# Stores on another queue and a divided last product in an encoder step

## The chip, the cores and the metric

The kernel runs on one core of one Trainium2 chip. The metric is device time in microseconds of one execution; the profiled execution is a further one, whose records give the span and the rows that are quoted. Engines are named as in the profile: PE multiplies matrices, PEld loads its weights, DVE, ACT and POOL work elementwise, SP issues transfers. SP and POOL each have a program of their own: an instruction that waits holds up everything behind it on the same engine.

## The reference

One layer of a streaming encoder over 2048 prompt frames and 64 sample frames of width 1024: a gated linear recurrence and a windowed attention are merged, multiplied by an output projection and added to the input; then a convolutional feed-forward network with a down projection, and a final RMS norm. The parts around the change are:

```python
def rmsnorm(x, g):
    x32 = x.astype(jnp.float32)
    y = x32 * lax.rsqrt(jnp.mean(x32 * x32, axis=-1, keepdims=True) + RMS_EPS)
    return (y * g.astype(jnp.float32)).astype(x.dtype)
...
        mixed = jax.nn.sigmoid(g_rnn) * y_rnn + jax.nn.sigmoid(g_attn) * y_attn
        x = x + mixed @ w_out[l]
        xn2 = rmsnorm(x, norm_ffn[l])
        up = xn2 @ w_up[l]
        fbuf = jnp.zeros((b, FFN_CONV_W - 1, 2 * D_FF), x.dtype) if first else ffn_conv[l]
        up_c, fbuf_new = causal_dwconv(up, fbuf, ffn_conv_w[l], ffn_conv_b[l])
        gate, val = jnp.split(up_c, 2, axis=-1)
        x = x + (jax.nn.silu(gate) * val) @ w_down[l]
...
    y = rmsnorm(x, norm_final)
```

All is float32, with D_MODEL = 1024 and D_FF = 2816.

## The kernel before

Each float32 operand is split into a rounded part and a remainder (hi on ACT at L197, lo on DVE at L198), and each product is three matmuls: hi by hi, hi by lo, lo by hi. The 2112 frames are columns, cut into six blocks of 320, 320, 320, 320, 416 and 416; two of them are a pair, and PAIRS names the three pairs. SBUF is divided into regions (RA, RB, RC, RE, FW, FA, FB, FD and more), and the profile names tiles by their region: "RE<-woS" is a load of output-projection weights into RE.

The mixer (recurrence, attention) fills the first 1370 us. Three stages follow.

*Output projection, about 1373 to 1600.* Three phases, i = 0, 1, 2, one for each pair. In each, `wout(i, m)` makes eight row blocks m: it loads the residual of two tiles (L796, from xT), multiplies the mixed rows by the block's weights (`mm3`, L223 to L225: 48 matmuls), and `residual` adds (L811), squares (L815 or L818) and sums the squares (L819); the result goes to x1S in DRAM (L812). `wload(i, m)` gets the weights: in phase 0 from the input, split and stored to woS (L787); in phases 1 and 2 from woS (L780), 1 MB each into one of two buffers. `wload(i, m + 1)` stands after the matmuls in `wout`. Stores are put in a list, `stores`, and issued one `wout` later behind the next loads. `norms(i - 1)` makes the RMS factors of the pair before (L681 on PE, L682 on ACT, L683 on DVE) at m = 0. Beside all this a generator prepares the next pair's rows (`mixes`, loads at L772) and the feed-forward operands of a finished pair (`xprep`, loads of x1S at L733); `drive(beside, n)` lets it take n steps for each m.

*Up projection and convolution, about 1600 to 2555.* Products of a Strassen-like scheme, seven in place of eight, over 22 groups of rows and three pairs (a plan lists which lanes run together). Up weights are combined, split and stored for the next pass (wuS, L853) or loaded back; each lane's result goes through convolution and gate and is stored as operand of the down products (hS, L995).

*Down projection, about 2555 to 3022.* `seq` lists seven products by three pairs by 11 steps; each step loads one token tile of hS (`dtoken`, L1079), splits it, and does twelve matmuls (L1305 to L1307). The last product of the first pair, (6, 0), comes at the end and is done in two passes over its 11 steps, rows 0 and 1 and then rows 2 and 3; the second pass loads and splits the same 11 tiles again. Generators in `side`, driven one step after each product step, add the residual, square (L1276), sum (L1277), and write the outputs: `outputs` makes the RMS factor (L681 to L683), multiplies each of eight row blocks (L1286) and stores it (L1287).

No scheduler reorders this: the order on an engine is the order in which the Python code calls it, with the generators interleaved and a helper that delays some operations by a number of products (`later`). Every store and load of the whole kernel is issued by SP.

## Time and profile before

| | |
|---|---|
| median of 3 runs | 3022.07 us (3018.11 to 3022.51) |
| profiled execution | 3023.75 us, span 3022.0 us |
| PE busy | 2883.6 us, 95% |
| DVE, ACT, POOL busy | 2173.0, 1520.8, 146.2 us |
| granted TensorE clock | 0.98 |
| transfers | 581.14 MB, mean 192 GB/s |
| chain that ended last | PE 70%, DVE 11%, DMA 9%, ACT 3% |

The largest transfers that the change touches, from the page's list of issues (out <- in, issuing queue, count, KB each, median us from issue to landing):

```profile
hS<-FA SPq DMA_DIRECT2D x154, 160.0 KB, 3.1
hS<-FB SPq DMA_DIRECT2D x77, 208.0 KB, 4.2
woS<-RB SPq DMA_DIRECT2D x8, 1024.0 KB, 6.2
x1S<-FW SPq DMA_DIRECT2D x32, 160.0 KB, 5.5
out_yT_dram<-RR SPq DMA_DIRECT2D x32, 160.0 KB, 2.9
```

How to read rows: a group has line, engine, operation, tiles and count, then busy us and mean ns, then idle time ahead of it with what ended it. In waits the thing behind the arrow is what came last. "SPq" is time of SP's instruction stream, waits included, and a busy PE counts as busy at the slow clock too.

### The profile page before, as it was taken

The page shows a single profiled execution, that of the slowest core. Times are in us where ns is not written, and L with a number is a line of the kernel's source. Part 1 is how long each engine was busy: PE and PEld are TensorE (multiplying, and loading weights), DVE is VectorE, ACT ScalarE, POOL GpSimd, SP SyncE. Part 2 cuts the span into 40 slices and gives each one's busy share as a digit, 9 for nine tenths or more (in the row PEclk, how much of TensorE's full clock was granted, in tenths as well). Part 3 has the DMA queues.
Part 4 walks back from the last instruction along what each step waited for, and adds up shares of the span by engine and source line. Part 5 has one row for each costly group of instructions (what it writes and reads, how often), then busy time and mean ns, then how long its engine had stood idle before and what let it go on. Part 6 is the DMA issues. An engine that isn't in the chain of part 4 may idle for free.

```text
span 3022.0 us, 48591 instructions
## 1 busy us (share of the span) xinstructions
PE 2883.6 (95%) x17572; PEld 2797.1 (93%) x17572; DVE 2173.0 (72%) x4220; ACT 1520.8 (50%) x3427; POOL 146.2 (5%) x104
## 2 busy tenths in 40 slices
PE   8989999999999999999899999999699999999997
PEld 7989888999998999998799999999599999899997
DVE  5398884378786288886568888888866767566776
ACT  4466662366663366664325555555444545334442
POOL 3221112000000000000000000000000000000000
PEclk9999999999999999999899999999899999999998
DMA  7875537543335643338875555545767666976653
GB/s 240 279 233 179 188 134 232 193 134 125 124 122 167 201 138 129 125 106 279 274 245 204 183 176 179 177 166 189 252 213 240 225 229 217 269 215 203 210 171 125
DMA packets 340914, 581.14 MB, mean 192 GB/s; under 512 B 35169, under 2 KB 263841, under 8 KB 320705
## 3 DMA queue, kind: packets, MB, share of 16 engines
q1 hardware_dynamic: 340672, 578.04, 58.3%
q8 instruction: 138, 2.26, 0.3%
q14 instruction: 104, 0.84, 0.1%
HBM read 393.26 MB, written 185.18 MB: 191 GB/s over the span
## 4 chain that ended last, share of the span: by engine, by line
PE 70%; DVE 11%; DMA 9%; ACT 3%; issue 2%; SPq 1%; POOL 0%; DVEq 0%; ACTq 0%; POOLq 0%
PE mm L224 8%; PE mm L223 8%; PE mm L225 8%; PE mf L913 6%; PE mf L914 6%; PE mf L915 6%; PE mm L913 4%; PE mm L915 4%; PE mm L914 4%; PE mf L1306 2%; PE mf L1307 2%; PE mf L1305 2%; PE pt L467 1%; PE mm L1306 1%; PE mm L1307 1%
## 5 line engine op out<-in xcount | busy, mean ns | idle before, releaser
L223 PE MATMUL mm<-xh,whl 128*128 128x320 f32 (+2 forms) x2112 | 689.8, 327 | 8.7 <-ACT xh L197 5.6
L224 PE MATMUL mm<-xl,whl 128*128 128x320 f32 (+2 forms) x2112 | 688.3, 326 | 8.5 <-DVE xl L198 4.8
L225 PE MATMUL mm<-xh,whl 128*128 128x320 f32 (+2 forms) x2112 | 684.9, 324 | 0.8 <-POOL whl L198 0.8
L197 ACT ACTIVATE RE<-FW 128x512 fp32r<-128x512 f32 (+2 forms) x585 | 320.1, 562 | 446.9 <-DMA FW<-hS 68.7
L198 DVE TENSOR_TENSOR RE<-FW,RE 128x512 fp32r<-128x512 f32 (+2 forms) x585 | 344.4, 604 | 182.6 <-ACT RE L197 164.7
L224 PEld LDWEIGHTS mm<-xl,whl 128*128 128x128 f32 x2112 | 400.8, 190 | 17.8 <-DVE xl L198 8.2
L223 PEld LDWEIGHTS mm<-xh,whl 128*128 128x128 f32 x2112 | 401.1, 190 | 16.2 <-ACT xh L197 8.0
L225 PEld LDWEIGHTS mm<-xh,whl 128*128 128x128 f32 x2112 | 401.1, 190 | 1.8 <-POOL whl L198 1.1
L1306 PE MATMUL mf<-RE 128*128 128x320 f32 (+1 forms) x594 | 192.4, 324 | 1.9 <-DVE RE L198 1.8
L1305 PE MATMUL mf<-RE 128*128 128x320 f32 (+1 forms) x594 | 192.7, 325 | 0.0
L1307 PE MATMUL mf<-RE 128*128 128x320 f32 (+1 forms) x594 | 191.0, 322 | 0.0
L913 PE MATMUL mf<-RE 128*128 128x320 f32 (+1 forms) x472 | 155.0, 330 | 19.3 <-ACT RE L197 15.1
L949 DVE SCALAR_TENSOR_TENSOR FW<-FA,pkt,FW 128x640 f32<-128x640 f32 x176 | 154.4, 879 | 10.9 <-ACT FW L943 8.0
L915 PE MATMUL mf<-RE 128*128 128x320 f32 (+1 forms) x472 | 153.4, 326 | 2.1 <-DVE RE L198 2.1
L914 PE MATMUL mf<-RE 128*128 128x320 f32 (+1 forms) x472 | 154.1, 327 | 0.4 <-DVE RE L198 0.4
L913 PE MATMUL mm<-RE 128*128 128x320 f32 (+1 forms) x408 | 132.5, 325 | 5.6 <-DVE FA L966 2.8
L913 PE MATMUL mf<-RA,RE 128*128 128x320 f32 (+1 forms) x416 | 136.8, 329 | 0.0
L914 PE MATMUL mf<-RA,RE 128*128 128x320 f32 (+1 forms) x416 | 136.2, 327 | 0.0
L915 PE MATMUL mf<-RA,RE 128*128 128x320 f32 (+1 forms) x416 | 135.8, 326 | 0.0
L915 PE MATMUL mm<-RE 128*128 128x320 f32 (+1 forms) x408 | 131.5, 323 | 4.0 <-DVE RE L198 4.0
L914 PE MATMUL mm<-RE 128*128 128x320 f32 (+1 forms) x408 | 131.5, 322 | 0.0
L454 ACT ACTIVATE pr<-S,nm 128x256 f32<-128x256 f32 (+1 forms) x272 | 123.4, 472 | 7.5 <-DVE nm L450 6.0
(336 smaller groups left out, 7059.8 us busy)
## 6 DMA issues: line engine op xcount, KB each, us to landing
whl<-wiS SPq DMA_DIRECT2D x88, 1024.0 KB, 5.1
RE<-wuS SPq DMA_DIRECT2D x96, 512.0 KB, 4.3
wiS<-whl SPq DMA_DIRECT2D x44, 1024.0 KB, 4.8
wuS<-RE SPq DMA_DIRECT2D x88, 512.0 KB, 2.7
FW<-in_w_up_dram SPq DMA_DIRECT2D x160, 256.0 KB, 3.4
FW<-in_w_dn_dram SPq DMA_DIRECT2D x121, 256.0 KB, 4.1
FW<-hS SPq DMA_DIRECT2D x165, 160.0 KB, 3.3
hS<-FA SPq DMA_DIRECT2D x154, 160.0 KB, 3.1
```

Of the source, the lines that this page charges most:

```text
L197: nc.scalar.activation(hi, src, AF.Copy)
L198: (lo_eng or nc.vector).tensor_tensor(lo, src, hi.bitcast(F32), op=ALU.subtract)
L223: nc.tensor.matmul(ps[:, :n], wh[:, c], xh[:, k, :n], start=first, stop=False)
L224: nc.tensor.matmul(ps[:, :n], wh[:, c], xl[:, k, :n], start=False, stop=False)
L225: nc.tensor.matmul(ps[:, :n], wl[:, c], xh[:, k, :n], start=False, stop=last)
L913: nc.tensor.matmul(ps[:, :n], w[:, 0, c], x[:, k, 0], start=first, stop=False, **more)
L914: nc.tensor.matmul(ps[:, :n], w[:, 0, c], x[:, k, 1], start=False, stop=False, **more)
L915: nc.tensor.matmul(ps[:, :n], w[:, 1, c], x[:, k, 0], start=False, stop=last, **more)
L949: nc.vector.scalar_tensor_tensor(uc, G[:, j:j + self.cols], col("fw", 44 * j + m), uc, op0=ALU.mult, op1=ALU.add)
L1305: nc.tensor.matmul(ps[m][:, :n], w[:, 0, c], t[:, 0], start=k == 0, stop=False)
L1306: nc.tensor.matmul(ps[m][:, :n], w[:, 0, c], t[:, 1], start=False, stop=False)
L1307: nc.tensor.matmul(ps[m][:, :n], w[:, 1, c], t[:, 0], start=False, stop=k == 10)
```

## The change

Ten kinds of stores move from SP's queue to POOL's: the final states h, lc and fc, woS, x1S, wuS, hS, s2S, the sums rS, and the outputs yT. POOL has no other work after the mixer. The list of delayed stores disappears, so each store is issued where its result is made. `wload(i, m + 1)` moves to the start of `wout`, ahead of the residual's loads. `norms(i - 1)` moves to m = 1, and phase 2's generator takes no steps at m = 0 and 1 and three afterwards, in place of two each time.

The last product keeps its 11 token tiles after the first pass. Four of them are loaded and split early, at step (6, 1, 3), into buffers of up weights that are free by then (`wh`). Rows 2 and 3 are done in two column halves of 160 in place of one pass of 320; squares and outputs follow by column slice, and `outputs` yields three more times before its RMS factor.

```diff
-            stores.append(lambda: nc.sync.dma_start(woS[m], t.bitcast(F32)))
+            nc.gpsimd.dma_start(woS[m], t.bitcast(F32))
...
     def wout(i, m):
         w, work = weights.pop((i, m)), []
+        if m < 7:
+            wload(i, m + 1)
...
-        due = stores[:]
-        stores.clear()
-        if m < 7:
-            wload(i, m + 1)
-        for f in due:
-            f()
...
-            stores.append(lambda t0=t0, n=n, xr=xr: nc.sync.dma_start(x1S[m, :, t0:t0 + n], xr))
+            nc.gpsimd.dma_start(x1S[m, :, t0:t0 + n], xr)
...
-                nc.sync.dma_start(wuS[g, i], t.bitcast(F32))
+                nc.gpsimd.dma_start(wuS[g, i], t.bitcast(F32))
...
-                nc.sync.dma_start(hS[ORDER.index(o), g % 11, :, OFF[p]:OFF[p] + n], src)
+                nc.gpsimd.dma_start(hS[ORDER.index(o), g % 11, :, OFF[p]:OFF[p] + n], src)
...
-        t = dr.tile([P, 2, BM], F32R, name="hh")[:, :, :n]
+        t = (wh.tile([P, 2, 4 * P], F32R, name="wh") if spare else dr.tile([P, 2, BM], F32R, name="hh"))[:, :, :n]
...
-    seq += [(6, 0, k, r) for r in (range(2), range(2, 4)) for k in range(11)]
+    seq += [(6, 0, k, r, c) for r, c in ((range(2), slice(0, 320)), (range(2, 4), slice(0, 160)),
+                                         (range(2, 4), slice(160, 320))) for k in range(11)]
...
-            toks[j] = dtoken(prods[i][1], p, k)
+            if (i, p, k) not in toks:
+
+                toks[i, p, k] = dtoken(prods[i][1], p, k, (i, p) == (6, 0) and k < 4)
...
-            if i and m == 0:
+            if i and m == 1:
                 norms(i - 1)
...
-            drive(beside, (2, 4, 2)[i])
+            drive(beside, (2, 4, 3)[i] if i < 2 or m > 1 else 0)
...
-    def outputs(p, c):
+    def outputs(p, c, cs=None):
         b, n = PAIRS[p][c == "2"]
-        r = rms(ssum[b], n, ssum[b])
+        cs = cs or slice(0, n)
+        s = ssum[b][:, cs]
+        for _ in range(3):
+            yield
+        r = rms(s, cs.stop - cs.start, s)
...
-            nc.sync.dma_start(yT[m * P:(m + 1) * P, b:b + n], y)
+            nc.gpsimd.dma_start(yT[m * P:(m + 1) * P, b + cs.start:b + cs.stop], y)
...
+        if (i, p, k) == (6, 1, 3):
+            for jj in range(4):
+                fetch(len(seq) - 33 + jj)
```

SP at the end of phase 0, before (L772 mixed rows, L796 residual, L787 and L780 store and load of woS, L812 store of x1S):

```order
L772 DMA FW<-mixS 128x320 x2
L787 DMA woS<-RB 128x2048
L796 DMA FW<-in_xT_dram 128x320 x2
L812 DMA x1S<-FW 128x320 x2
L772 DMA FW<-mixS 128x320 x2
L780 DMA RE<-woS 128x2048
L812 DMA x1S<-FW 128x320 x2
L796 DMA FW<-in_xT_dram 128x320 x2
L780 DMA RE<-woS 128x2048
L772 DMA FW<-mixS 128x416 x2
```

And SP there in the changed kernel:

```order
L796 DMA FW<-in_xT_dram 128x320
L780 DMA RE<-woS 128x2048
L772 DMA FW<-mixS 128x320
L785 DMA FW<-in_w_out_dram 128x512
L796 DMA FW<-in_xT_dram 128x320
L772 DMA FW<-mixS 128x320
L785 DMA FW<-in_w_out_dram 128x512
L796 DMA FW<-in_xT_dram 128x320
L772 DMA FW<-mixS 128x320
L780 DMA RE<-woS 128x2048
L785 DMA FW<-in_w_out_dram 128x512
```

Both of phase 1's first loads of woS now stand among the loads of phase 0's own weights (L785), and no store stands in the queue.

DVE in the tail, before (L198 splits of token tiles, L1277 and L683 sums and RMS factor, L1333 sums of products, L1286 outputs):

```order
L683 RECIPROCAL FD<-FD 128x416
L1277 TENSOR_TENSOR FD<-FD 128x320
L1286 SCALAR_TENSOR_TENSOR RR<-RR,pkt,FD 128x416 x8
L683 RECIPROCAL FD<-FD 128x320
L198 TENSOR_TENSOR RE<-FW,RE 128x320
L1286 SCALAR_TENSOR_TENSOR RR<-RR,pkt,FD 128x320 x8
L198 TENSOR_TENSOR RE<-FW,RE 128x320 x5
L1333 TENSOR_TENSOR RR<-mm,RR 128x320 x2
```

And in the changed kernel, where the lines are L1272 for the sums, L1335 for the sums of products and L1285 for the outputs:

```order
L683 RECIPROCAL FD<-FD 128x416
L1272 TENSOR_TENSOR FD<-FD 128x320
L1285 SCALAR_TENSOR_TENSOR RR<-RR,pkt,FD 128x416 x8
L683 RECIPROCAL FD<-FD 128x320
L1335 TENSOR_TENSOR RR<-mm,RR 128x320
L1285 SCALAR_TENSOR_TENSOR RR<-RR,pkt,FD 128x320 x8
L1335 TENSOR_TENSOR RR<-mm,RR 128x320
L1272 TENSOR_TENSOR FD<-FD 128x320 x2
```

No split stands between or behind the outputs any more; the last rows then come as two groups of 160 columns, each with its own sums, factor and eight outputs.

POOL's last rows in the changed kernel:

```order
L1286 DMA out_yT_dram<-RR 128x320 x16
L1286 DMA out_yT_dram<-RR 128x416 x16
L1286 DMA out_yT_dram<-RR 128x320 x8
L1286 DMA out_yT_dram<-RR 128x160 x16
```

These stores were SP's; the last eight of 320 columns are now sixteen of 160.

More of the change, by code (lines that the diff above doesn't have):

```diff
@@ L1066, in dweight @@
             nc.vector.tensor_tensor(t, c, t, op=ALU.subtract)
-            nc.sync.dma_start(s2S[k], t)
+            nc.gpsimd.dma_start(s2S[k], t)
         else:
@@ L1151 @@
             wload(i + 1, 0)
-            while stores:
-                stores.pop(0)()
             io[i].close()
@@ L1214 @@
             if i == 0:
-                while stores:
-                    stores.pop(0)()
                 for t0, n in PAIRS[2]:
-                    nc.sync.dma_start(rS[:, t0:t0 + n], rsum[t0])
+                    nc.gpsimd.dma_start(rS[:, t0:t0 + n], rsum[t0])
                 io[2].close()
@@ L1265, in resid, with squares @@
             yield
-    def squares(p, q, ms=range(4)):
+    def squares(p, q, ms=range(4), cs=None):
         b, n, rows = quarter(p, q)
+        cs = cs or slice(0, n)
         for m, y in [rows[m] for m in ms]:
@@ L1358 @@
         if i == 6:
-            side.append(squares(p, "21", ms))
+            side.append(squares(p, "21", ms, cs))
             if ms[-1] == 3:
-                side.append(outputs(p, "1"))
+                side.append(outputs(p, "1", cs))
     drive(side, 999)
-    nc.sync.dma_start(fc_o, fx.rearrange("p a b c -> p (a b c)"))
+    nc.gpsimd.dma_start(fc_o, fx.rearrange("p a b c -> p (a b c)"))
     for region in (FD, RR, FW, RE):
```

37 lines of the change are left out of this document (19 added, 18 removed).

## Prediction

> **What bounds the kernel now.** I read the program stage by stage first, because the change touches four places that together are a small part of it. The view is busy time by stretch: from and to in us, the length, the busy time of PE, PEld, DVE, ACT and POOL with instruction counts, the granted TensorE clock, the DMA engines' busy share and GB/s.
>
> ```profile
> 1373.00:1440.00 67.00, 62.00 (x384) 58.73 (x384) 36.33 (x75) 28.07 (x58) 0.00 (x0) 0.95 0.93 320
> 1440.00:1450.00 10.00, 3.48 (x8) 1.83 (x8) 6.71 (x8) 3.88 (x7) 0.00 (x0) 0.65 0.91 292
> 1450.00:1520.00 70.00, 61.68 (x386) 60.95 (x385) 40.60 (x90) 24.01 (x52) 0.00 (x0) 0.93 0.78 261
> 1520.00:1600.00 80.00, 75.78 (x388) 73.33 (x387) 50.78 (x101) 22.70 (x46) 0.00 (x0) 0.98 0.72 237
> 1620.00:2100.00 480.00, 480.00 (x3273) 479.83 (x3273) 409.57 (x656) 256.75 (x578) 0.00 (x0) 1.00 0.50 175
> 2100.00:2210.00 110.00, 78.76 (x403) 70.81 (x402) 93.54 (x156) 51.87 (x106) 0.00 (x0) 0.84 0.76 252
> 2540.00:2640.00 100.00, 95.56 (x586) 91.55 (x585) 63.57 (x112) 40.32 (x87) 0.00 (x0) 1.00 0.85 255
> 2640.00:2940.00 300.00, 299.14 (x1833) 296.42 (x1832) 204.17 (x401) 121.06 (x245) 0.00 (x0) 1.00 0.66 198
> 2940.00:3022.00 82.00, 63.98 (x376) 61.58 (x374) 51.72 (x97) 23.53 (x52) 0.00 (x0) 0.88 0.44 138
> ```
>
> In the bulk of the ConvFFN (the rows from 1620 and from 2640) PE is busy 99.7% to 100%: whatever moves there is worth nothing while the stores still come in time. What can be won lies in the output projection (1373 to 1600), at the turn 2100 to 2210, a little at 2540, and in the tail. Next, what PE waits for after 1358 (line, releaser; total us, times, longest), and what SP's queue waits for in the projection:
>
> ```profile
> PE mf L913 <- ACT RE L197: 15.1, 3, 9.6
> PE mf L223 <- DMA RE<-woS: 12.3, 6, 4.2
> PE mm L1306 <- DVE RE L198: 7.0, 3, 4.5
> PE mf L913 <- DMA RE<-wuS: 4.2, 1, 4.2
> PE mm L223 <- DMA RE<-woS: 3.9, 2, 3.7
> ```
>
> ```profile
> SPq L796 <- DMA x1S<-FW: 39.8, 18, 5.0
> SPq L812 <- DVE FW L811: 16.6, 13, 4.3
> ```
>
> PE waits 16.2 us for the projection's weights (woS). SP, which issues every load and store in program order, stands 56 us still: 16.6 us until a result to be stored exists (L812), and 39.8 us at L796, a load of the residual whose buffer is still being stored. The weight loads stand behind these. At the end of phase 0 this is seen whole, first SP, then PE (start, duration, what; the wait before it in brackets):
>
> ```profile
> 1440.64 0.38 SPq L780 DMA_DIRECT2D RE<-woS  x1
> 1442.77 3.02 SPq L796 DMA_DIRECT2D FW<-in_xT_dram  x2
> 1445.83 0.48 SPq L780 DMA_DIRECT2D RE<-woS  x1
> ```
>
> ```profile
> 1442.95 2.46 PE L681 MATMUL mf<-FW,ones 128*128 128x320 f32 x4 [2.82 <-DVE FW L819]
> 1449.12 0.63 PE L223 MATMUL mm<-RE 128*128 128x320 f32 x1 [3.71 <-DMA RE<-woS]
> 1449.56 0.47 PE L224 MATMUL mm<-RE 128*128 128x320 f32 x1
> 1452.76 0.47 PE L224 MATMUL mm<-RE 128*128 128x320 f32 x1
> 1454.03 0.31 PE L225 MATMUL mm<-RE 128*128 128x320 f32 x1
> 1454.17 0.31 PE L223 MATMUL mm<-RE 128*128 128x320 f32 x1
> ```
>
> PE first waits 2.82 us for the sums of squares, then 3.71 for the weights. A stall costs more than its idle time: from 1449.56 to 1452.76 lie twelve starts, 0.267 us each, while at 1454 a start follows 0.14 to 0.15 us after another. At the slow pace until about 1453.3, some 16 matmuls lose 16 x 0.12 = 1.9 us.
>
> **The change, part by part.** All durations are from the profiled execution, 3023.75 us with a span of 3022.0, 1.7 above the median of the runs; the sum is made against 3023.75.
>
> *Projection, turn from phase 0 to 1.* Stores leave SP, wload comes first in wout, and norms moves from m = 0 to m = 1. In the new order two RE<-woS loads stand among phase 0's loads, some 20 rows before the phase's last; the first now starts at 1440.64, one landing too late. Removed: 2.82 + 3.71 idle and 1.9 of slow pace, 8.4 us. The four L681 are not removed, only put behind 48 matmuls. I take -8.
>
> *Phases 1 and 2.* The same view of PE's waits, for 1450 to 1530 and for 1530 to 1620:
>
> ```profile
> PE mf L223 <- DMA RE<-woS: 8.3, 3, 4.2
> PE mf L223 <- DMA RE<-woS: 4.0, 3, 3.4
> ```
>
> That is 12.3 us, and by the 1.9 above I estimate 1.5 of slow pace behind each of the three waits of over 3 us. SP's 5 us holds disappear as its cause, but the DMA share is 0.78 and 0.72 over the stages, so some loads are late for want of bytes. Bounds: 0 and -12.3 - 4.5 = -17; I take half, -6 for phase 1 and -3 for phase 2, as the share is nearer to 0.75 than to the 0.93 of phase 0.
>
> *Phase 0 pays.* Two loads of 1 MB move from its end into a phase at 0.93 and 320 GB/s: 2 MB / 320 GB/s = 6.5 us of transfer. PE had 5 us idle in 67 there. Bounds 0 (they fill gaps) and +6.5; I take +3.
>
> *The issue itself.* No store before is POOL's, so its price c per store is unknown. Rows near it: one issue of SP, above 0.38 (L780, one instruction), and POOL's own work:
>
> ```profile
> L198 POOL TENSOR_TENSOR gl<-gr,gh 128x256 fp32r<-128x256 f32 x24 | 21.1, 880 | 802.2 <-ACT gh L197 666.2 <-DMA qr<-qS 136.0
> L198 POOL TENSOR_TENSOR whl<-wraw,whl 128x1024 fp32r<-128x1024 f32 x30 | 75.5, 2520 | 241.6 <-ACT whl L197 205.2 <-PE mm L225 20.6 <-PE pt L467 15.8
> ```
>
> So 0.38 to 2.52 us, and I take the short POOL instruction, 0.88. In the bulk this is hidden: POOL is idle after 1358 (0.00 in all rows above), and wuS and hS stores, some 320 in the 950 us from 1600, come one in 3 us, so that even 2.52 keeps pace. The largest of them are these (KB each, us to landing):
>
> ```profile
> wuS<-RE SPq DMA_DIRECT2D x88, 512.0 KB, 2.7
> ```
>
> A later store frees its buffer later, and what covers that are the other buffers of the ring; if they didn't, each of the 88 would stand on PE with c, +77 at 0.88. I take 0. No gain is possible there, since PE is full.
>
> *Turn 2100 to 2210.* DVE is busy 93.5 of 110 us, so most of PE's 15.1 (L913 for an ACT split of a late operand) stays. The 4.2 of RE<-wuS is a load behind SP's stores. Bounds +2 (x1S stores later by one or two c) and -6; I take -2.
>
> *Start of the down products, 2540 to 2640.* 4.4 us idle at a DMA share of 0.85. s2S and hS stores leave the loads' queue, the bytes stay: -1 (0 to -3).
>
> *Tail.* Here DVE's order and PE's form change:
>
> ```profile
> 2984.78 4.58 DVE L1286 SCALAR_TENSOR_TENSOR RR<-RR,pkt,FD 128x416 f32<-128x416 f32 x8
> 2991.68 3.77 DVE L1286 SCALAR_TENSOR_TENSOR RR<-RR,pkt,FD 128x320 f32<-128x320 f32 x8
> 3012.98 2.15 DVE L683 RECIPROCAL FD<-FD 128x320 f32<-128x320 f32 x1 [1.46 <-ACT FD L682]
> 3015.17 3.79 DVE L1286 SCALAR_TENSOR_TENSOR RR<-RR,pkt,FD 128x320 f32<-128x320 f32 x8
> ```
>
> ```profile
> 2991.82 0.64 PE L1306 MATMUL mm<-RE 128*128 128x320 f32 x1 [4.49 <-DVE RE L198]
> 2995.91 0.63 PE L1306 MATMUL mm<-RE 128*128 128x320 f32 x1 [2.13 <-DVE RE L198]
> ```
>
> ```profile
> 2992.00:2999.00 7.00, 4.87 (x17) 4.47 (x18) 5.47 (x13) 0.47 (x1) 0.00 (x0) 0.50 0.70 231
> 2999.00:3009.00 10.00, 9.98 (x66) 9.71 (x66) 5.72 (x13) 4.47 (x11) 0.00 (x0) 0.97 0.45 136
> ```
>
> The splits (L198) of the kept rows now all stand ahead of these outputs, so PE's 4.49 + 2.13 go, and 17 matmuls in 4.87 us become 17 x 0.15 = 2.6, another 2.3. Against it the second half is 132 matmuls of 160 columns, and PE does not get twice as fast. Matmuls of 128 columns run like this:
>
> ```profile
> 129.87 0.28 PE L441 MATMUL S<-kA,D 128*128 128x128 f32 x1
> 130.09 0.28 PE L441 MATMUL S<-kA,D 128*128 128x128 f32 x1
> ```
>
> with one L442 between, 0.11 us each. So 160 columns take between 0.11 and 0.15: at 0.112, 14.8 us against 9.98 for 66. PE ends 8.9 - 4.8 = 4.1 us earlier. Behind it the reciprocal (2.15 at 320) and the eight products (3.79) work on 160 columns. From 416 to 320 columns eight products fall by 0.8 us, so 160 columns are about 2.5 us, the reciprocal about 1.2, the adds some 0.3 less: 2.5 us saved, but the first half's outputs now stand ahead on DVE (+0.6). DVE ends 4.1 + 2.5 - 0.6 = 6 us earlier, at 3018.96 - 6 = 3013. Then the stores. POOL issues 32 of them from 2985.4 on (2984.78 and an eighth of 4.58). Its last 16 can start when the first column half is done: PE's first rows end at 2999 - 8.9, 66 x 0.112 behind that is 2997.5, and from the last matmul to the first product pass 3015.7 - 3009.4 = 6.3 us now, so about 3003.5. Behind the last product now follow 3022.0 - 3018.96 = 3.0 us, 0.4 of it the issue and 2.6 the landing. The span ends at the latest of 3013 + c, 3003.5 + 16c and 2985.4 + 32c, plus 2.6:
> c = 0.38: 3016, -6. c = 0.88: 3020.2, -2. c = 1.05: 3021.6, 0. c = 1.3: 3029.6, +7.6. c = 2.52: 3068.6, +47. I take -2.
>
> The Trainium skill, page "DMA: Bandwidth & Descriptors", section "Specifications", gives about 1 us to the first byte of a DMA whose descriptors GpSimd writes and about 0.6 for one from the sync queue: by that the last landing alone would come 0.4 us later, an estimate from that page that no run here shows yet.
>
> *Sum.* -8 - 6 - 3 + 3 - 2 - 1 - 2 = -19: 3023.75 - 19 = 3005.
>
> **Rivals.**
>
> *Bytes set the projection.* If the woS loads are late because 16 DMA engines are full, an earlier issue only trades one late transfer for another. For it: 0.91 and 0.93 in the first two rows of the first view. Against it: after 1450 the share falls to 0.78 and 0.72, and SP idles 39.8 us at L796 in the same stretch. Then phase 0's +3 to +6 eats the turn's gain, and -3 to -5 in all is left: about 3019. The Trainium skill, same page, section "Issuing engines are not separate DMA queues", speaks for this: DMAs of all issuers run on the same 16 engines, and a second issuer saves only the sequencer's time, usually small. The trace has that time as 39.8 and 16.6 us of waiting, which is not small.
>
> *POOL's issue is the new bound (slower).* One mechanism: stores are issued serially on POOL at c, and the last 32 stand in one row at the end. With the other terms at -17 the break-even is 2985.4 + 32c + 2.6 = 3022 + 17, c = 1.6 us. For it: POOL's instructions take 0.88 to 2.52 us, all above SP's 0.38. Against it: a 160-column store is a small piece. At c = 1.8, 3045.6 - 3022 = +23.6, so 3023.75 - 17 + 23.6 = 3030; at 2.0, 3037.
>
> *All of it works.* The woS waits go wholly with their slow pace (-8.4 - 12.3 - 4.5), the turn gives -4, the start of the down products -2, c is 0.38 and the tail -6: -37, 2987.
>
> *The change doesn't do what it says* can't be for the stores, which stand on POOL in the new order; it can for phase 2's loads, since they still stand behind L796 loads that wait for a store four buffers back, now POOL's. This is part of the first rival.
>
> **How the numbers follow.** My forecast has 0.50, bytes 0.20, all of it 0.14, POOL's issue 0.16. This kernel's measurement can tell about 0.2%, 6 us, so "faster" means below 3016. The forecast (its own range 2996 to 3014) and the larger gain are faster, 0.64, and a fifth of the bytes case, 0.04: 0.68. Of the rest of that case 0.15 is within 0.2% and 0.01 beyond, which with POOL's 0.16 makes 0.17 slower. The range runs from 2988, between the larger gain and the forecast, to 3030, the nearer half of POOL's case: about 0.2 is left out.
>
> **What would show it right or wrong.** Right: the two waits of PE around 1442 and 1449 are gone, and the first RE<-woS begins at least 8 us before its use; PE's waits for woS fall from 16.2 us to below 8; L796 waits below 20 us; in the tail the waits of 4.49 and 2.13 are gone, 160-column matmuls start about 0.11 us apart, and POOL's stores follow each other under 1.05 us. Wrong: POOL's last stores are issued in one row that begins before DVE's last products and ends well after; or PE's waits for woS stay at the same DMA share; or PE leaves 100% in the bulk, waiting for a buffer that a late store holds.

## The result and the profile after

The changed kernel takes 3035.2 us (median of six runs, 3030.5 to 3037.2), the kernel before in the same comparison 3022.4 (3018.1 to 3027.1). The ratio is 1.004 with a 95% interval of 1.0027 to 1.0053: 12.8 us slower. The forecast was 3005 us, 19 faster; the time lies above the range too. The profiled execution of the changed kernel took 3036.2 us with a span of 3034.4, against 3022.0 before.

The page of the changed kernel, PE's busy time and the shares of the chain that ended last:

```profile
PE 2888.3 (95%) x17640; PEld 2804.9 (92%) x17640; DVE 2167.6 (71%) x4222; ACT 1513.2 (50%) x3418; POOL 386.1 (13%) x551
...
PE 57%; issue 20%; DVE 10%; DMA 3%; POOL 3%; ACT 3%; POOLq 0%; SPq 0%; DVEq 0%; ACTq 0%
```

PE's share of the chain fell from 70% to 57%; "issue" (2% before) has 20% and POOL 3%. This is a hint to the place and not the price: of two kernels below that lose the same, one has 15% of "issue" and the other 1% (b_wu_pool, b_wu_pool8). Where the 12.4 us of span were lost is read from rows that both programs have. On DVE these are the last residual of the projection (L811 before, L805 after), the "128x64" product of the last pair's convolution that first follows the turn (L991, L985), the same row of the last group, and the first-pass adds of the last product (L1333, L1335). The timeline of before, then of after (start, duration, what; in brackets the wait):

```profile
1600.63 0.58 DVE L811 SCALAR_TENSOR_TENSOR FW<-mf,FW 128x416 f32<-128x416 f32 x1
...
2229.51 0.22 DVE L991 SCALAR_TENSOR_TENSOR FB<-FB 128x64 f32<-128x64 f32 x1
...
2551.89 0.22 DVE L991 SCALAR_TENSOR_TENSOR FB<-FB 128x64 f32<-128x64 f32 x1
...
2978.04 1.37 DVE L1333 TENSOR_TENSOR RR<-mf,RR 128x320 f32<-128x320 f32 x3 [1.20 <-PE mf L1307]
```

```profile
1598.17 0.58 DVE L805 SCALAR_TENSOR_TENSOR FW<-mf,FW 128x416 f32<-128x416 f32 x1
...
2238.70 0.23 DVE L985 SCALAR_TENSOR_TENSOR FB<-FB 128x64 f32<-128x64 f32 x1
...
2563.45 0.22 DVE L985 SCALAR_TENSOR_TENSOR FB<-FB 128x64 f32<-128x64 f32 x1
...
2993.99 1.37 DVE L1335 TENSOR_TENSOR RR<-mf,RR 128x320 f32<-128x320 f32 x3 [1.01 <-PE mf L1306]
```

The projection ends 2.5 us earlier. From there to the row behind the turn, which I call the up stretch, the changed kernel takes 640.5 us in place of 628.9 (+11.6); from that row to the last group's 324.8 in place of 322.4 (+2.4, all of it in the last group: 39.1 in place of 36.8); the down products 430.5 in place of 426.2 (+4.4); the tail 40.4 in place of 44.0 (-3.6). The projection and the tail give back 6, and the feed-forward network in between loses 18.

Busy time by stretch in the changed kernel (columns as in the prediction's first view):

```profile
1373.00:1440.00 67.00, 58.41 (x334) 55.62 (x334) 32.05 (x68) 25.68 (x55) 9.70 (x18) 0.87 0.94 332
1440.00:1450.00 10.00, 9.34 (x51) 9.08 (x52) 5.40 (x12) 2.85 (x6) 2.69 (x5) 0.83 0.74 267
1450.00:1520.00 70.00, 60.65 (x382) 59.52 (x381) 43.63 (x90) 25.93 (x54) 8.09 (x15) 0.93 0.73 243
...
1620.00:2100.00 480.00, 478.79 (x3263) 478.13 (x3262) 408.28 (x653) 254.45 (x575) 111.49 (x208) 1.00 0.49 173
2100.00:2210.00 110.00, 73.83 (x386) 66.14 (x384) 90.36 (x150) 47.66 (x94) 16.07 (x30) 0.86 0.72 244
2540.00:2640.00 100.00, 91.36 (x537) 88.49 (x535) 62.78 (x108) 41.52 (x93) 10.25 (x19) 0.97 0.79 244
```

The turn of the phases (1440) is filled, 9.34 of 10 us in place of 3.48. The bulk stays nearly full (478.79 of 480). The losses stand where PE had gaps before: 73.83 in place of 78.76 at the turn, 91.36 in place of 95.56 at the start of the down products. What PE waits for after 1358:

```profile
PE mf L223 <- DMA RE<-woS: 10.1, 4, 6.1
PE mf L1305 <- DVE RE L198: 6.2, 3, 4.0
...
PE mf L907 <- DMA RE<-wuS: 5.1, 1, 5.1
PE mm L1305 <- DVE RE L198: 4.8, 3, 2.2
```

POOL's own groups (line, engine, operation, tiles, count; busy us, mean ns; idle before, releaser), and the transfers by issuing queue (KB each, median us from issue to landing):

```profile
L989 POOL DMA_DIRECT2D hS<-FA x154 | 82.7, 541 | 228.5 <-DVE FA L982 152.9 <-DVE FA L1002 37.3 <-DVE FA L993 32.2
L853 POOL DMA_DIRECT2D wuS<-RE x88 | 47.1, 536 | 257.4 <-DVE RE L198 255.7
L1286 POOL DMA_DIRECT2D out_yT_dram<-RR x56 | 29.9, 539 | 368.2 <-DVE RR L1285 357.7 <-DVE RR L1335 10.1 <-issue 0.2
```

```profile
wuS<-RE POOLq DMA_DIRECT2D x88, 512.0 KB, 4.1
hS<-FA POOLq DMA_DIRECT2D x154, 160.0 KB, 4.0
hS<-FB POOLq DMA_DIRECT2D x77, 208.0 KB, 5.0
x1S<-FW POOLq DMA_DIRECT2D x32, 160.0 KB, 4.3
```

One store costs POOL 0.54 us, whether it is 80, 160 or 512 KB, less than the 0.88 I took. But the feed-forward stores land later: wuS 4.1 us after its issue in place of 2.7, hS 4.0 and 5.0 in place of 3.1 and 4.2. Only x1S lands earlier, 4.3 in place of 5.5, and that is the new order's work and not the queue's: from SP, in the run a_all_sp2 below, it is 2.9.

One sentence ahead of the prediction needs mending. It says that no scheduler reorders the program and that the order on an engine is the order of the Python calls. The traces show otherwise: when eight wuS stores alone go from SP to POOL (run b_wu_pool8 below), 24 rows of DVE and 6 of ACT stand at other places, although no call on these engines moved. Two executions of one program (a_all_sp and a_all_sp2) differ in none. A store's queue thus also changes how the other engines' work is ordered, and part of what follows can't be parted from that.

### The profile page after: what moved, and what is told of

It is laid out like the page before. It is cut to its first block, busy times and chain, and to the rows that moved or that the text cites. A ratio compares the mean times of both kernels' runs of the same rounds, so it can differ in the third digit from the quotient of the medians.

```text
span 3034.4 us, 48959 instructions
## 1 busy us (share of the span) xinstructions
PE 2888.3 (95%) x17640; PEld 2804.9 (92%) x17640; DVE 2167.6 (71%) x4222; ACT 1513.2 (50%) x3418; POOL 386.1 (13%) x551
## 4 chain that ended last, share of the span: by engine, by line
PE 57%; issue 20%; DVE 10%; DMA 3%; POOL 3%; ACT 3%; POOLq 0%; SPq 0%; DVEq 0%; ACTq 0%
PE mm L224 8%; PE mm L223 8%; PE mm L225 8%; PE mf L908 3%; PE mf L909 3%; PE mf L907 3%; PE mf L1304 3%; PE mf L1306 3%; PE mf L1305 3%; PE mm L908 2%; PE mm L909 2%; PE mm L907 2%; POOL hS L989 2%; PE mm L1305 1%; PE mm L1304 1%
## 5 line engine op out<-in xcount | busy, mean ns | idle before, releaser
L198 DVE TENSOR_TENSOR RE<-FW,RE 128x512 fp32r<-128x512 f32 (+2 forms) x574 | 340.3, 608 | 171.9 <-ACT RE L197 166.3
L224 PEld LDWEIGHTS mm<-xl,whl 128*128 128x128 f32 x2112 | 399.8, 189 | 18.7 <-DVE xl L198 8.5
L223 PEld LDWEIGHTS mm<-xh,whl 128*128 128x128 f32 x2112 | 400.6, 190 | 16.6 <-ACT xh L197 8.2
L1305 PE MATMUL mf<-RE 128*128 128x320 f32 (+2 forms) x616 | 198.1, 322 | 6.2 <-DVE RE L198 6.2
L1304 PE MATMUL mf<-RE 128*128 128x320 f32 (+2 forms) x616 | 199.4, 324 | 0.0
L1306 PE MATMUL mf<-RE 128*128 128x320 f32 (+2 forms) x616 | 197.4, 320 | 0.0
L907 PE MATMUL mf<-RE 128*128 128x320 f32 (+1 forms) x472 | 156.8, 334 | 23.1 <-ACT RE L197 13.5
L908 PE MATMUL mf<-RE 128*128 128x320 f32 (+1 forms) x472 | 155.6, 330 | 1.1 <-DVE RE L198 1.0
L909 PE MATMUL mf<-RE 128*128 128x320 f32 (+1 forms) x472 | 154.6, 328 | 0.0
```

Source lines behind the costliest of these rows:

```text
L198: (lo_eng or nc.vector).tensor_tensor(lo, src, hi.bitcast(F32), op=ALU.subtract)
L223: nc.tensor.matmul(ps[:, :n], wh[:, c], xh[:, k, :n], start=first, stop=False)
L224: nc.tensor.matmul(ps[:, :n], wh[:, c], xl[:, k, :n], start=False, stop=False)
L907: nc.tensor.matmul(ps[:, :n], w[:, 0, c], x[:, k, 0], start=first, stop=False, **more)
L908: nc.tensor.matmul(ps[:, :n], w[:, 0, c], x[:, k, 1], start=False, stop=False, **more)
L909: nc.tensor.matmul(ps[:, :n], w[:, 1, c], x[:, k, 0], start=False, stop=last, **more)
```

## The experiments

The theory after the result: the stores of the feed-forward network (wuS, hS, s2S) land later from POOL, and where buffers are scarce somebody waits for the landing. The rivals: POOL's issue time; the new order of the projection and the tail; something that any second queue would do. All times below are against the kernel before in the same comparison. "Up", "group", "down" and "tail" are the stretches defined above, in us, from each run's profile.

| run | stores on POOL, other edits | ratio (95%) | up | group | down | tail |
|---|---|---|---|---|---|---|
| before | | | 628.9 | 36.8 | 426.2 | 44.0 |
| the change | all | 1.004 (1.0027-1.0053) | 640.5 | 39.1 | 430.5 | 40.4 |
| a_ffn_sp | x1S, woS, yT | 0.9986 (0.9976-0.9997) | 631.2 | 36.8 | 425.5 | 42.4 |
| b_ffn_pool | wuS, hS, s2S alone | 1.0062 (1.0048-1.0076) | 641.1 | 38.5 | 428.8 | 44.9 |
| b_tail | none, last product | 0.9986 (0.9974-0.9998) | 627.4 | 36.6 | 425.4 | 38.9 |
| a_all_sp | final states, order, last product | 0.9979 (0.9967-0.9991) | 629.4 | 36.1 | 425.6 | 38.7 |
| a_all_sp2 | the same again | 0.9962 (0.9949-0.9975) | 628.7 | 36.4 | 424.0 | 38.4 |
| a_proj_pool | x1S, woS, order, last product | 0.9963 (0.9945-0.998) | 631.5 | 36.3 | 428.1 | 38.4 |
| a_order | final states, order | 0.9991 (0.9982-1.0001) | 628.4 | 37.1 | 424.3 | 44.3 |
| b_wu_pool | 88 wuS | 1.0026 (1.0016-1.0036) | 637.5 | 36.3 | 425.1 | 44.4 |
| b_wu_pool8 | 8 wuS | 1.0025 (1.0013-1.0037) | 636.5 | 36.6 | 425.7 | 44.1 |
| b_wu_act | 88 wuS on ACT, one execution | | 631.6 | 36.1 | 422.4 | 43.7 |
| b_wu_act2 | the same again | 1.0004 (0.9993-1.0015) | 631.7 | 36.3 | 426.0 | 44.8 |
| b_hs_pool | 231 hS | 1.0016 (1.0004-1.0028) | 633.7 | 38.4 | 424.1 | 43.6 |
| b_hs_late | 231 hS, sums later | 1.0019 (1.001-1.0028) | 633.3 | 39.4 | 423.9 | 43.7 |
| b_late | sums later | 0.9988 (0.9979-0.9997) | 627.0 | 37.0 | 423.5 | 44.1 |
| b_s2_pool | 11 s2S | 1.0005 (0.9995-1.0016) | 628.2 | 36.4 | 428.1 | 44.2 |
| a_late_sp | a_all_sp, sums later | 0.996 (0.9945-0.9974) | 628.0 | 36.7 | 424.3 | 38.4 |
| a_wu8_sp | the change, 8 wuS on SP | 1.0035 (1.0023-1.0046) | 636.7 | 39.1 | 428.8 | 42.8 |
| a_wu8_hs_sp | and hS, s2S on SP | 1.0009 (0.9997-1.002) | 631.4 | 37.2 | 423.4 | 45.4 |

Two executions of one program tell how far to trust a stretch: a_all_sp and a_all_sp2 agree within 0.8 us in "up" and 1.6 in "down", but their projections end at 1599.2 and 1590.1. So the end of the projection is no measure of anything under 9 us here; for the projection the ratios count. The pair b_wu_act and b_wu_act2 agrees within 0.3 us in "up" and "group", but its "down" differs by 3.6 and its tail by 1.1: in "down" nothing under 4 us can be told.

### Undo the feed-forward stores, or do them alone

a_ffn_sp is the changed kernel with wuS, hS, s2S and rS on SP again, each by a line like the first pair here; b_ffn_pool is the kernel before with wuS, hS and s2S on POOL, by lines like the second pair.

```diff
-                nc.gpsimd.dma_start(wuS[g, i], t.bitcast(F32))
+                nc.sync.dma_start(wuS[g, i], t.bitcast(F32))
```

```diff
-                nc.sync.dma_start(wuS[g, i], t.bitcast(F32))
+                nc.gpsimd.dma_start(wuS[g, i], t.bitcast(F32))
```

> The changed kernel with the ConvFFN's stores (wuS, hS, s2S, rS) issued by SP again; the projection's stores (x1S, woS) and the outputs stay with POOL. Theory L (a store issued by POOL lands about 1 us later, and DVE and ACT wait in place for the buffer): the 8.3 us lost at 2100 to 2220 and the 8.4 us lost at 2500 to 2720 come back, 3035 - 16 = 3019, and DVE's wait of 10.5 us for hS at the start of the down products is gone. Rival O (the order of the projection's edits leaves the ConvFFN's operands late, whoever issues its stores): stays at 3035, both losses stay.

> The kernel before with only the ConvFFN's stores (wuS, hS, s2S) issued by POOL. Theory L: 3022 + 16 = 3038, with DVE waiting for hS. Rival O: 3022, no loss, since the projection's order is that of before.

Without them the changed kernel is faster than the one before, 0.9986; with them alone the kernel before is 1.0062. Both put the price of these 330 stores between 16 and 19 us (1.004 - 0.9986 = 0.0054, 16.3 us; 0.0062, 18.7), and in both most of the loss lies in "up" (9.3 us of it between the changed kernel and a_ffn_sp, 12.2 between the kernel before and b_ffn_pool), with 1.7 to 2.4 in "group". This settles where, not yet why.

### The last product and the order alone

b_tail is the kernel before with only the last product's new form, yT on SP; the core of it:

```diff
-    seq += [(6, 0, k, r) for r in (range(2), range(2, 4)) for k in range(11)]
+    seq += [(6, 0, k, r, c) for r, c in ((range(2), slice(0, 320)), (range(2, 4), slice(0, 160)),
+                                         (range(2, 4), slice(160, 320))) for k in range(11)]
```

a_all_sp, and a_all_sp2 once more, is the changed kernel with woS, x1S, wuS, hS, s2S, rS and yT on SP, each by a line like this one; a_proj_pool is the same, but for x1S and woS, which stay on POOL.

```diff
-            nc.gpsimd.dma_start(yT[m * P:(m + 1) * P, b + cs.start:b + cs.stop], y)
+            nc.sync.dma_start(yT[m * P:(m + 1) * P, b + cs.start:b + cs.stop], y)
```

a_order is a_all_sp with the last product as before, which leaves these edits, the stores without a list of delayed ones, and two of the three final states on POOL:

```diff
+        if m < 7:
+            wload(i, m + 1)
...
-            if i and m == 0:
+            if i and m == 1:
...
-            drive(beside, (2, 4, 2)[i])
+            drive(beside, (2, 4, 3)[i] if i < 2 or m > 1 else 0)
```

> The kernel before with only the last product's edit (tokens kept, four split early, second half in two column halves, outputs by slice), all stores with SP. Both theories: the tail alone gains 3 to 5 us, 3018; PE's waits of 4.5 and 2.1 us at 2990 are gone. If POOL's store price were what limited the tail of the changed kernel, this one would gain 6 or more.

> The changed kernel with all stores but the three states issued by SP, at the place where the changed kernel issues them: the order edits alone. Theory L: the ConvFFN's 16 us come back, the projection loses what the free SP queue gave, because SP then waits for each result (L805) ahead of its loads: 3020 to 3028. Rival O: 3035 or more, the losses at 2100 and 2500 stay.

> The changed kernel's order edits alone (weights loaded ahead of the residual, norms at m = 1, generator steps 2, 4, 3, each store issued where its result is made), with x1S, woS and the ConvFFN's stores on SP and the last product as before. Both theories: what the kernel with all stores on SP gains less what the last product alone gains, 7.7 - 4.6, so 3 us faster than before. If the projection's gain needs the second queue, it is 0 or slower.

> The kernel with the order edits and the last product's edit and all stores on SP once more, beside before in the same runs: 6 to 9 us faster than before (0.997 to 0.998), and faster than the order edits alone by the 4 to 5 us of the tail.

> The changed kernel with only the projection's stores (x1S, woS) issued by POOL, all others by SP. Against the kernel with all stores on SP (3011.8 beside 3019.5 before) it tells what the second queue is worth in the projection: if SP's waits for its own stores set the woS loads, 5 to 10 us faster than that, 3002 to 3007; if the ring of four residual tiles and the two weight buffers set them whoever stores, within 2 us of it, 3010 to 3014.

The last product's new form is worth 4.2 us (0.9986), and 5.1 to 5.6 in its stretch (44.0 to 38.9 or 38.4). The order of the projection is worth 2.7 us at 0.9991, with an interval that ends at 1.0001. Both with every store but the final states on SP give 0.9979 and 0.9962, 6 and 11 us. That x1S and woS are POOL's changes nothing that can be told: 0.9963 against those two. The second queue, which the change is mostly about, gives nothing in the projection's time, though it does move the loads. With the stores on SP (a_order, a_all_sp, a_all_sp2) phase 1's first load of woS starts at 1439 to 1445, and PE waits 7.1 to 8.4 us for it at the turn of the phases. With x1S and woS on POOL (the change, a_proj_pool) it starts at 1405 to 1407 and that wait is gone. But PE then waits 5.6 to 6.1 us for the third load, and 2.4 to 4.5 us for ACT at 1614 to 1616. Why the third load is late is seen in SP's waits of the changed kernel from 1373 to 1600, and in its timeline at the start of phase 1:

```profile
SPq L796 <- DMA x1S<-FW: 68.4, 28, 5.5
```

```profile
1463.33 0.43 SPq L780 DMA_DIRECT2D RE<-woS  x1
...
1467.68 5.71 SPq L796 DMA_DIRECT2D FW<-in_xT_dram  x2
```

SP no longer waits for results to store, so it runs ahead until L796 finds the residual's four buffers full: 68.4 us at that line, in place of 39.8. The weight loads still stand behind it. The one of 1463.33 is too late, and PE's longest wait for woS is 6.1 us. A larger ring for the residual would be the next step; it was not tried.

### Which of the stores

From the kernel before, one kind each: b_wu_pool moves wuS (L859), b_hs_pool hS (L995), b_s2_pool s2S (L1067), by a line like the second of the b_ffn_pool pair above. b_wu_pool8 moves only the eight wuS of groups 10 and 21:

```diff
-                nc.sync.dma_start(wuS[g, i], t.bitcast(F32))
+                (nc.gpsimd if g % 11 == 10 else nc.sync).dma_start(wuS[g, i], t.bitcast(F32))
```

> The kernel before with only the 88 wuS stores issued by POOL. Theory L (later landing, met by a wait in place): ACT's splits into the ring of four up-weight buffers wait for the store, which shows where products are single (2100 to 2160): about 5 to 8 us slower, 3025 to 3027, the loss between 2100 and 2220 only, DMA to landing 4.0 us in place of 2.7. Rival S (POOL's issue time itself, 0.54 us a store, or the bytes of a second queue cost it): 88 stores of the 319 cost their share everywhere they lie, 1620 to 2555, in proportion: 4 us spread over the bulk, and PE leaves 100% there.

> The kernel before with only the 231 hS stores issued by POOL. Theory L: DVE's sums that overwrite a stored half (L1003) wait for its store where the last groups meet the first down products: 5 to 8 us slower, most of it after 2540, DVE's wait for hS there about 10 us in place of none. Rival S: 12 us spread over 1620 to 2640.

> The kernel before with only the 11 s2S stores on POOL. wuS and hS alone lost 4 us each in the profile, all of it before 2250, and the three together 15, of which 4 to 5 came after 2500. Theory: the s2S stores cost that, 3 to 5 us, at 2570 to 2640, where a w_dn load waits for the buffer that s2S is stored from. Rival: nothing alone; the late loss needs hS and s2S together, DVE's wait for hS (7 us, hidden when alone) taking the cover from the other.

> The kernel before with 8 of the 88 wuS stores on POOL, those of the two last groups of up rows (10 and 21), whose products come singly at 2095 to 2125; the other 80 stay with SP. Theory T (only the stores at the turn cost, because ACT's next split waits there for one of them to land): nearly the whole loss of all 88 on POOL, 5 to 8 us slower, and ACT's waits for wuS of 2 and 3.4 us are there. Theory S (every store on POOL costs a little, by its issue or by sharing): 8/88 of it, under 1 us.

In the kernel before, 88 wuS stores cost 0.26%, and eight of them, at the turn, cost the same 0.25%. So the other 80 cost nothing that can be told: it is not the issue, which all 88 have, but a place. The 231 hS cost 0.16%, the 11 s2S by themselves nothing that can be told.

At the turn ACT makes the hi half of each new up weight in a ring of four buffers, and a buffer comes free when its wuS store has landed. The timeline of ACT from 2105 to 2150, its splits that waited for that, before, then b_wu_pool8, then the changed kernel:

```profile
2126.65 0.63 ACT L197 ACTIVATE RE<-FW 128x512 fp32r<-128x512 f32 x1 [1.52 <-DMA wuS<-RE]
```

```profile
2119.51 0.63 ACT L197 ACTIVATE RE<-FW 128x512 fp32r<-128x512 f32 x1 [3.20 <-DMA wuS<-RE]
2139.03 0.63 ACT L197 ACTIVATE RE<-FW 128x512 fp32r<-128x512 f32 x1 [3.61 <-DMA wuS<-RE]
```

```profile
2113.21 0.63 ACT L197 ACTIVATE RE<-FW 128x512 fp32r<-128x512 f32 x1 [1.78 <-DMA wuS<-RE]
2130.49 0.63 ACT L197 ACTIVATE RE<-FW 128x512 fp32r<-128x512 f32 x1 [2.51 <-DMA wuS<-RE]
```

ACT's 1.5 us become 6.8 and 4.3. In b_wu_pool8 the start of the loss can be followed row by row. ACT's splits and the first copy out of PE's results (L960) behind them are shown before and then in b_wu_pool8, and last the PE row there that waits for the next such copy (all from 2105 to 2150):

```profile
2108.93 1.21 ACT L197 ACTIVATE RE<-FW 128x512 fp32r<-128x512 f32 x2 [0.18 <-DVE FW L866]
2110.05 0.42 ACT L960 ACTIVATE FA<-mm 128x320 f32<-128x320 f32 x1
```

```profile
2115.68 0.63 ACT L197 ACTIVATE RE<-FW 128x512 fp32r<-128x512 f32 x1 [0.18 <-DVE FW L866]
...
2120.04 0.42 ACT L960 ACTIVATE FA<-mm 128x320 f32<-128x320 f32 x1
```

```profile
2121.74 0.41 PE L913 MATMUL mm<-RA,RE 128*128 128x320 f32 x1 [2.92 <-ACT FA L960]
```

Up to the first split these rows, and the results of the turn's first five wuS, stand 6.7 us later than before, most of it from the projection, which ended 6.3 us later in this execution. The next split is the one that waits 3.20 us, for a store that landed 7.0 us after its issue in place of 3.9. The copy behind it comes another 3.2 us late, PE waits 2.92 us in place of 0.53, and the sixth result is 2.4 us later still. Here the late landing itself starts the loss; the rest of the 7.6 us that "up" loses in this run was not followed as closely. Further on PE waits for the loads that bring these weights back (RE<-wuS): between 2080 and 2230 it is 10.4 us in b_wu_pool8 and 9.2 in the changed kernel, in place of 5.4. In the bulk the same store lands about as late (4.0 us is the median of all 88 in b_wu_pool), but there PE stays full.

What hS costs in "up", 4.8 us in b_hs_pool, was not followed. DVE's waits for hS from 1600 to 2230 grow from 9.5 to 36.3 us, but only 4.4 of them lie at the turn, from 2080 on, in place of 3.2.

### Is it POOL, or any second queue

b_wu_act, and b_wu_act2 once more, is the kernel before with wuS issued by ACT:

```diff
-                nc.sync.dma_start(wuS[g, i], t.bitcast(F32))
+                nc.scalar.dma_start(wuS[g, i], t.bitcast(F32))
```

> The kernel before with the 88 wuS stores issued by ACT, a queue of its own that isn't POOL's. If the later landing is that of POOL's kind of queue, it is 2.7 us here as on SP; if it is that of any second queue beside SP's loads, it is about 4 us as on POOL. The time itself is not the question, since ACT waits for DVE ahead of each store.

> wuS issued by ACT once more, beside before. Its stores land 3.9 us after issue (median), as late as on POOL (4.0), and ACT issues nothing while it waits for DVE. If the landing alone made the loss: 3 to 8 us slower, as on POOL. If what counts is the moment at the turn when ACT may go on (the last store issued there came at 2115 in place of 2121 to 2124): not slower than before.

The first, one execution, took 3013.97 us, the second comes out at 1.0004 (0.9993 to 1.0015), not slower as far as that can tell. From the list of transfers of b_wu_act2, and ACT's waits there:

```profile
wuS<-RE ACTq DMA_DIRECT2D x88, 512.0 KB, 3.9
```

```profile
2113.02 0.63 ACT L197 ACTIVATE RE<-FW 128x512 fp32r<-128x512 f32 x1 [0.31 <-DMA wuS<-RE]
2117.08 0.63 ACT L197 ACTIVATE RE<-FW 128x512 fp32r<-128x512 f32 x1 [0.17 <-DMA wuS<-RE]
```

By the median of all 88 the later landing is no property of POOL: from ACT it is 3.9 us, and from POOL 4.0 to 4.1. But at the turn, where it counts, the eight stores land after 3.6 us from ACT (median), 3.1 from SP before, and 4.3 from POOL (b_wu_pool and b_wu_pool8; 3.8 in the changed kernel). So ACT's run is not one with POOL's late landing and without its loss: ACT waits 0.5 us for the ring in place of 6.8. Nor is it plainly without loss, for "up" is 2.7 to 2.8 us longer than before in both executions, which the interval of the ratio, up to 1.0015 or 4.5 us, leaves room for. The order of the other engines changes far more here than in b_wu_pool8 (hundreds of rows on DVE and on ACT), so that this run can't part the landing from the order.

### The waits of DVE for hS, and the sums one product later

DVE's sums of Strassen operands are made in place, in FB, from which hS is stored. DVE's waits from 2500 to 2640 in the changed kernel, then the first of them in its timeline:

```profile
DVE FW L1059 <- DMA FW<-in_w_dn_dram: 22.3, 8, 4.5
DVE FB L997 <- DMA hS<-FB: 10.5, 3, 4.2
```

```profile
2535.49 0.59 DVE L997 TENSOR_TENSOR FB<-FB 128x416 f32<-128x416 f32 x1 [4.23 <-DMA hS<-FB]
```

The same views before, where L1003 is the changed kernel's L997 and L1065 its L1059:

```profile
DVE FW L1065 <- DMA FW<-in_w_dn_dram: 7.3, 4, 3.0
DVE FW L1062 <- DMA FW<-in_w_dn_dram: 7.3, 5, 2.8
...
DVE FB L1003 <- DMA hS<-FB: 1.7, 1, 1.7
```

The wait for hS grows from 1.7 to 10.5 us. That for down weights grows less than one line says: with a third row of 2.7 it was 17.3 in all before, beside 22.3. And b_s2_pool has 26.8 of it without a loss that can be told. I tried to part the two by making each sum, and its stores, one product later: b_late is the kernel before with this edit alone, b_hs_late has hS on POOL beside it, a_late_sp is the edit on a_all_sp.

```diff
-                at(3, sums_a)
-                at(4, lambda: store("T1", h[:, :n]))
+                at(4, sums_a)
+                at(5, lambda: store("T1", h[:, :n]))
...
-                at(4, sums_b)
-                at(5, lambda: (sums_c(), store("T2", self.e[:, :n]), store("T3", self.e[:, n:])))
-                at(6, lambda: store("T4", h[:, :n]))
+                at(5, sums_b)
+                at(6, lambda: (sums_c(), store("T2", self.e[:, :n]), store("T3", self.e[:, n:])))
+                at(7, lambda: store("T4", h[:, :n]))
```

> The kernel with only the hS stores on POOL, and every sum that overwrites a stored half asked for one product later (sums_a, sums_b, sums_c and the stores of their results). Theory L: DVE finds the store landed, its wait for hS at the start of the down products (7.4 us) falls below 2, and of the 5 to 7 us that the hS stores cost on POOL 3 or more come back: 3020 to 3024 beside 3020 before. Rival P (the changed place of the stores makes the scheduler order loads and splits otherwise, and that costs, not the landing): stays at 3025 to 3028.

> The control: the kernel before with the same sums one product later, all stores on SP. By theory L there is little to gain, since its store lands in time there: within 3 us of before, 3017 to 3023. If it gains as much as the one with the stores on POOL, the later sums are worth something by themselves and that run says nothing on the landing.

> Order edits, last product's edit and the later sums of the control together, all stores on SP: if the three gains add (3, 4.6 and 3.6 us), 10 to 12 us faster than before, 3007 to 3010; if the later sums only moved a wait, the same as without them, 3008 to 3012.

The experiment failed in its aim: b_hs_late keeps 6.7 us of the wait and its loss, 1.0019. By the edit the store of T1 and the sum that overwrites its tile both move by one product, so their distance stays. On SP the edit alone shows 0.9988, but on top of a_all_sp it adds nothing (0.996 beside 0.9962), so I don't count on it. Sums that are not made in place would settle this; it was not tried.

### Put them back, one after another

a_wu8_sp is the changed kernel with the eight wuS of groups 10 and 21 back on SP; a_wu8_hs_sp has hS and s2S back too.

```diff
-                nc.gpsimd.dma_start(wuS[g, i], t.bitcast(F32))
+                (nc.sync if g % 11 == 10 else nc.gpsimd).dma_start(wuS[g, i], t.bitcast(F32))
...
-                nc.gpsimd.dma_start(hS[ORDER.index(o), g % 11, :, OFF[p]:OFF[p] + n], src)
+                nc.sync.dma_start(hS[ORDER.index(o), g % 11, :, OFF[p]:OFF[p] + n], src)
...
-            nc.gpsimd.dma_start(s2S[k], t)
+            nc.sync.dma_start(s2S[k], t)
```

> The changed kernel with only the 8 wuS stores of the two last groups back on SP. If these 8 make the loss at the turn in the changed kernel as well: 6 to 8 us of its 12.6 come back, 1.002 in place of 1.004 against before, and ACT's waits for wuS of 4.3 us at 2110 to 2130 are below 2. If not: 1.004.

> The changed kernel with these 8 wuS stores, all hS and all s2S stores on SP; the other 80 wuS stores, x1S, woS and yT stay with POOL. If stores on POOL cost only where something waits for their landing: as fast as with all of the ConvFFN's stores on SP, 0.998 to 0.999 (3014 to 3018). If each store on POOL costs: 2 to 4 us slower than that.

Both fell short. Eight wuS back on SP take 3.8 us from "up" (640.5 to 636.7) and hardly anything from the time (1.0035 in place of 1.004, within the intervals). ACT waits 1.2 us for wuS, less than before the change, but PE's waits from 2100 to 2225 in a_wu8_sp have a new one:

```profile
PE mf L907 <- ACT FA L976: 4.6, 1, 4.6
```

Late is now ACT's convolution result (L976), another link of the same thin place. ACT's wait for the ring is thus not the price by itself: in a_wu8_hs_sp it is 3.3 us, with an "up" of 631.4. With hS and s2S back as well "up" is 631.4, "group" 37.2 and "down" 423.4, almost the figures of a_ffn_sp; and the waits at the start of the down products are gone. PE's two waits at L1305, 6.2 and 4.8 us in the changed kernel's list above, are 2.1 together in a_wu8_hs_sp, from 2500 to 2720:

```profile
PE mf L1305 <- DVE RE L198: 1.4, 5, 0.4
...
PE mm L1305 <- DVE RE L198: 0.7, 2, 0.4
```

So in the changed kernel's "up" stretch, taken off in this order, the eight wuS account for 3.8 us, hS with s2S for 5.3, the other 80 wuS for 0.2, and the rest up to 2.3 is what x1S and woS on POOL leave over against before. That a_wu8_hs_sp is still at 1.0009 fits the tail of its profile, 45.4 us.

### The tail

With the new last product the tail is 38.4 to 38.9 us in the five runs whose yT is issued by SP, and 40.4, 42.4, 42.8 and 45.4 in the four where POOL issues it. DVE's last products and POOL's stores in the changed kernel:

```profile
3019.55 2.46 DVE L1285 SCALAR_TENSOR_TENSOR RR<-RR,pkt,FD 128x160 f32<-128x160 f32 x8
...
3026.17 2.46 DVE L1285 SCALAR_TENSOR_TENSOR RR<-RR,pkt,FD 128x160 f32<-128x160 f32 x8
```

```profile
3022.81 8.50 POOL L1286 DMA_DIRECT2D out_yT_dram<-RR  x16 [10.08 <-DVE RR L1335]
```

The first result exists at about 3019.9, POOL begins at 3022.81 and stands in one row until 3031.31, 2.7 us after DVE's end; on SP (b_tail) the span ends 3.9 us after DVE's last product, here 5.8. Such late starts come again: in a_wu8_sp POOL begins its last eight 2.9 us after the first of their results. In both it begins 0.8 us after the last of DVE's eight products, while in a_wu8_hs_sp it begins 0.3 us after the first. And in a_wu8_hs_sp the last store is issued by 3009.7 and the transfers end near 3011, but the span ends at 3018.0. What POOL does in those gaps the trace doesn't show. What yT on POOL costs is read best from a_ffn_sp and a_proj_pool, which differ in yT alone: 0.9986 beside 0.9963, or 7 us with intervals that overlap a little, and a tail of 42.4 beside 38.4.

## Why the prediction was wrong

*"The issue itself. I take 0."* This is the step that failed. The issue is hidden, as it said: 0.54 us per store, and a bulk of 478.8 us in 480. But the sentence behind it, that a later store frees its buffer later and the ring covers that, was priced for the bulk alone, as all (77 us) or nothing. The right price was by place. At the turn and at the start of the down products PE was already waiting, so no slack was left there for 0.8 to 1.4 us per store. And I had put the lateness down to c, when the landing itself gets longer. Measured, the term that was put at 0 is +16 to +19 us.

*Turn 2100 to 2210, -2 with bounds of +2 and -6.* The row of PE's 4.2 us was read as a load behind SP's stores, and so as a gain. These loads bring back weights that were just stored, and PE's waits for them grew from 5.4 to 9.2 us. Measured: from the last bulk row (DVE's product at L988, L982 after the change, at 2099.79 and 2101.65) to the row behind the turn 137.1 us in place of 129.7, +7.3; outside the bounds. Only the x1S stores were counted as possible losers, not the wuS stores. The rest of the +11.6 comes from 1600 to 1620 (about 3.5; one wait of 4.5 us for ACT at 1616) and 1 from the bulk.

*Start of the down products, -1 (0 to -3).* +2.4 in the last group, where DVE waits for the landing of hS, in place; hS alone on POOL gives 1.6 of it (38.4). The +4.4 behind is hardly beyond the 3.6 by which two executions of one program differ there. hS alone shows none of it (424.1), and s2S alone +1.9, which can't be told. That DVE's later work for the down weights follows from the wait for hS is argued and not shown.

*Projection, -8 - 6 - 3 + 3 = -14.* The single steps are seen: the two waits at 1442 and 1449 are gone (9.34 of 10 us busy), PE's waits for woS are gone after 1530, and phase 0 pays (58.41 in place of 62.00 in its 67 us). That the first load comes early needs the queue; the order alone still waits 8.4 us at the turn (a_order). Phase 1 gained nothing: 10.1 us of waits in place of 8.3, since L796 holds SP as it did. That loads would still stand behind L796 was named, as a part of the bytes rival and for phase 2; it decided phase 1, and by the ring rather than by bytes, for the DMA share there is 0.73. In the whole projection PE's waits for woS fell to 10.1 us and SP's at L796 rose to 68.4, where I had named below 8 and below 20 as signs. x1S and woS on POOL make 0.9963, on SP 0.9962 and 0.9979. By the Trainium skill, page "DMA: Bandwidth & Descriptors", section "Issuing engines are not separate DMA queues", a second issuer saves only the sequencer's time, and these runs agree. I had set SP's waits of 39.8 and 16.6 us against it, but only the second is a matter of the queue. By the ratios the order is worth 2.7 us (a_order), or some 5 with what is over in a_all_sp and a_all_sp2, not 14: the steps were right, the size three to five times too large, since with the queue what is won at the turn is lost again in phases 0 and 1. By the ratios the gain doesn't come from the queue.

*Tail, -2.* -3.6 in the changed kernel, by the stated steps: the 4.49 and 2.13 are gone, the 160-column matmuls start 0.11 us apart, and DVE ends 6.3 us earlier after the first-pass adds (6 forecast). The term was too small since c is 0.54 and not 0.88. By the prediction's own formula 0.54 gives 3013 + 0.54 + 2.6 = 3016.1, or -6; some 2 us of that were lost because POOL's last row of stores began 2.9 us after the first result. (The formula was misread at c = 1.05, where its second term gives 3022.9 and not 3021.6; the forecast doesn't use that value.) By SP's queue the tail would have been 5.1 to 5.6 shorter. By the Trainium skill, same page, section "Specifications", the last landing would be 0.4 us later, an estimate from its two figures. The 80 KB outputs land 1.9 us after POOL's issue and, in a_all_sp2, 1.6 after SP's, so the trace nearly agrees in the quiet tail. The 1.4 us that wuS lost are more than that.

*The rival with the right sign*, POOL's issue as the bound, is wrong in its mechanism: c is far below its break-even of 1.6. One sign that I had given for it is there all the same: POOL's last stores stand in one row that begins before DVE's last products and ends 2.7 us after them. The cause is not c but the late start. "PE leaves 100% in the bulk, waiting for a buffer that a late store holds" was named as what would make the prediction wrong; it came true in the thin stages, not in the bulk (478.8 of 480 us).

The sum by measured terms: the new order and last product with stores on SP, about -9 (mean of -6.3 and -11.5); feed-forward stores on POOL, +16 to +19; yT on POOL, +2 to +4 by the tail and 7 by the ratios. That is +9 to +17, beside 12.8 measured. How much of the +16 is the landing and how much the changed order of ACT and DVE that comes with it stays open: b_wu_pool8 shows a loss of 2.4 us that begins at a late landing, and a_wu8_sp lost its waits without much gain.

The version that beats both kernels is the change with the ConvFFN's and the output's stores left on SP: 0.9962 to 0.9979 with x1S and woS on SP too, 0.9963 with them on POOL.

## What to carry to other kernels

A store that is given its own queue frees the engine that issued it, but may land later; before moving it, look who waits for its landing (a ring of buffers that is used again at once, a tile that is changed in place), and price that at the places where the bound engine already has gaps, not in the bulk. Move stores one kind at a time: here eight of 88 stores made the whole loss of their kind, as far as the intervals tell, and the gain came from two edits that needed no second queue. Where a queue only stood at a full ring, unloading it makes it wait longer at the ring, here 68.4 us in place of 39.8.
